# A hybrid GLA and Gated-DeltaNet layer: q and k of GLA as block pairs in seven products, gate dots inside the GDN heads, c spread by TensorE

## The chip, the cores and the metric

The kernel runs on one core of a Trainium2 chip. The metric is the device time of one execution in microseconds. The engines that matter are TensorE (PE, with its weight loads as PEld), VectorE (DVE), ScalarE (ACT), GpSimd (POOL) and SyncE (SP); SP and POOL also issue transfers, each in a queue of its own that it works through in order.

## The reference

The input x has 512 tokens of 2048 channels, c is one row of 2048. All is fp32.

```python
ada = silu(c) @ w_ada + b_ada              # shift, scale, gate: 3 x 2048
h = x * (1 + scale) + shift
q, k, v, g, ..., = split(h @ w_in)         # GLA, GDN, merge gates
# GLA: 4 heads, dk 256, dv 512: S_t = diag(a_t) S_{t-1} + k_t^T v_t, o_t = q_t S_t
# GDN: 16 heads, dk = dv = 128: S_t = a_t (I - b_t k_t k_t^T) S_{t-1} + b_t k_t v_t^T
y = sum over the two branches of sigmoid(merge) * (branch @ w_branch)
out = layernorm(x * alpha + gate * (y @ w_out))
```

What the change touches is the first part of GLA: q and k are each the product of h (512 x 2048) with a 2048 x 1024 matrix, and q is scaled by 1/16. It also touches the 48 tiles of ada: each of its values is a dot product of 2048 channels between silu(c) and one column of w_ada.

## The kernel before, in words

A fp32 product is built from three products of parts: each operand is split in a high part (rounded to the fast matmul's format) and the low rest, and `mm3` (L99 to L102) adds high by high, low by high and high by low. A tile of a projection is 128 output channels by 512 tokens: `proj_col` takes 16 contraction tiles of 3 matmuls, 48 of 512 columns.

Weights come in units of 512 KB (128 x 1024). `unit` (L71) loads a unit on SP's queue into `wraw` (3 buffers, L78), ACT casts it to `whi` (L86), and DVE subtracts to get `wlo` (L88); up to three units are made ahead of PE. Each engine works through its own instructions in order. The order within an engine is settled when the program is built, by a list scheduler that takes the order of the code as priority and a simulated readiness; buffers bound what may be in flight.

The stages, one after the other:

1. Start. silu(c) is spread over 128 partitions by a broadcast load and doubled on DVE (L209); each of the 32 values of shift and scale is a dot product of 2048 elements on DVE (L215) with a 1 MB tile of w_ada. h is made tile by tile: an affine on ACT, then the split (L94, L96). The first 32 steps run eight PSUM banks at a time in three groups of contraction tiles (`steps`, `made`).
2. GDN, 16 heads. `weave` runs a head's steps between the projections' matmuls. Per head: convolutions on DVE (L399, L403), a block solve of 31 rows on DVE (L667, L671) over the buffer `mi`, the state products, and 64 projection steps of PE that cover them. After the solve `mi` is free until the next head.
3. GLA, 4 heads: q and k (four `proj_col`, copied by ACT at L740 and L742), the decays (L746 to L754), the near part of the attention (L344, L350), the row projection of v, the levels (L840), the output, four gate tiles.
4. The gate of ada: 16 dots of 2048 (L215) with loads of 1 MB, between seven tiles of the merge projection.
5. The other merge tiles, the branch products, the output rows, the layer norm.

The projections of merge gates ("merge tiles") depend on h alone. Each ends with a tanh on ACT (L687) and a store to DRAM on SP (L688). A GDN head ends with a store of its output (L630).

## Time and profile before

| what | us |
|---|---|
| median of 3 runs | 2408.9 (2408.81 to 2409.92) |
| the profiled execution | 2410.16 |
| its span | 2408.4 |
| PE busy | 2367.4, 98% of the span, 11788 instructions |
| DVE busy | 1510.7, 63%, 2787 instructions |
| ACT busy | 1054.5, 44%, 1647 instructions |
| POOL busy | 80.3, 3%, 159 instructions |
| PE in the chain that ended last | 90% |

PE is busy from the first matmul to the last stage. The three halves of `mm3` on `pj` make 22, 21 and 21% of the chain that ended last. The granted clock of PE is at its upper level (2.4 GHz) in every one of the 40 slices. DMA is busiest in the first two slices and again in the last quarter, where the transfers of the gate's w_ada and the output rows fall. An idle time is given after an instruction in square brackets, with the engine and the tile that ended it.

### The profile page before, as it was taken

Reading aid. Unit: us, or ns where it says so; the run is one execution under the profiler, and the core shown is the slowest. Engines: PE = TensorE matmul, PEld = TensorE weight load, DVE = VectorE, ACT = ScalarE, POOL = GpSimd, SP = SyncE. Lnnn points to the kernel's source line nnn. Section 1 sums busy time; section 2 is a strip of 40 time slices with the busy share of each in tenths; the row PEclk is TensorE's granted clock in tenths of the full one; section 3 lists DMA queues with packets and bytes.
Section 4 is the critical chain, followed back from the end, with each engine's and each line's share of the span. In section 5 each row is a group of like instructions: output and inputs, shape, how many; then the busy total and the mean of one; then the engine's idle time right before and its main releaser. Section 6 shows DMA issues by size and latency. Waiting matters only on the chain.

```text
span 2408.4 us, 30754 instructions
## 1 busy us (share of the span) xinstructions
PE 2367.4 (98%) x11788; PEld 1943.4 (81%) x11788; DVE 1510.7 (63%) x2787; ACT 1054.5 (44%) x1647; POOL 80.3 (3%) x159
## 2 busy tenths in 40 slices
PE   6999999999999999999999999999999999999997
PEld 5888787888888888878888888888887888888886
DVE  7865677888777788873562745627475322344676
ACT  4335455555665555553442544425424311222353
POOL 0000000000000000000000000000002101010010
PEclk9999999999999999999999999999999999999999
DMA  9964333333333333233223222232298644445674
GB/s 393 369 216 136 114 100 100 100 100 102 100 100 103 108 104 96 96 96 119 94 75 110 88 91 88 76 114 88 92 350 284 214 140 138 146 147 184 215 246 148
DMA packets 119763, 347.92 MB, mean 144 GB/s; under 512 B 32448, under 2 KB 34880, under 8 KB 113472
## 3 DMA queue, kind: packets, MB, share of 16 engines
q1 hardware_dynamic: 109696, 313.45, 38.4%
q0 software_dynamic: 9920, 32.51, 3.9%
q8 instruction: 92, 1.51, 0.3%
q14 instruction: 55, 0.45, 0.1%
HBM read 318.57 MB, written 27.34 MB: 144 GB/s over the span
## 4 chain that ended last, share of the span: by engine, by line
PE 90%; DVE 4%; DMA 3%; issue 1%; ACT 1%; SPq 0%; POOL 0%; POOLq 0%; ACTq 0%; DVEq 0%
PE pj L100 22%; PE pj L101 21%; PE pj L102 21%; PE ms L158 2%; PE ms L157 2%; PE ms L159 2%; PE pj L133 2%; PE pj L134 2%; PE pj L135 2%; PE ms L100 1%; PE ms L102 1%; PE ms L101 1%; PE ms L840 1%; DVE junk L215 1%; DVE wlo L88 1%
## 5 line engine op out<-in xcount | busy, mean ns | idle before, releaser
L100 PE MATMUL pj<-acth,whi 128*128 128x512 f32 x2160 | 870.2, 403 | 20.8 <-ACT acth L94 19.2
L101 PE MATMUL pj<-acth,wlo 128*128 128x512 f32 x2160 | 845.2, 391 | 2.7 <-DVE wlo L88 2.7
L102 PE MATMUL pj<-actl,whi 128*128 128x512 f32 x2160 | 842.8, 391 | 0.0
L88 DVE TENSOR_TENSOR wlo<-wraw,whi 128x1024 fp32r<-128x1024 f32 x414 | 505.1, 1221 | 430.7 <-ACT whi L86 422.6
L86 ACT CAST whi<-wraw 128x1024 fp32r<-128x1024 f32 x414 | 433.7, 1048 | 585.4 <-PE pj L102 383.6
L100 PEld LDWEIGHTS pj<-acth,whi 128*128 128x128 f32 x2160 | 406.7, 188 | 101.4 <-ACT acth L94 20.0
L102 PEld LDWEIGHTS pj<-actl,whi 128*128 128x128 f32 x2160 | 405.9, 188 | 87.4 <-DVE actl L96 0.4
L101 PEld LDWEIGHTS pj<-acth,wlo 128*128 128x128 f32 x2160 | 407.0, 188 | 78.2 <-DVE wlo L88 4.1
L667 DVE TENSOR_TENSOR tmp<-vi,mi 128x8 f32<-128x8 f32 (+30 forms) x496 | 145.9, 294 | 13.3
L671 DVE TENSOR_REDUCE vi<-tmp 128x4 f32<-128x8 f32 (+30 forms) x496 | 111.1, 224 | 13.1
L215 DVE SCALAR_TENSOR_TENSOR junk<-wada,cs 128x2048 f32<-128x2048 f32 x48 | 109.7, 2285 | 4.7 <-DMA wada<-in_wada_dram 4.3
L100 PE MATMUL pj<-yh,whi 128*128 128x512 f32 x256 | 100.9, 394 | 0.0
L101 PE MATMUL pj<-yh,wlo 128*128 128x512 f32 x256 | 100.9, 394 | 0.0
L102 PE MATMUL pj<-yl,whi 128*128 128x512 f32 x256 | 100.9, 394 | 0.0
L158 PE MATMUL ms<-wlo,yh 128*128 128x512 f32 x240 | 94.8, 395 | 0.5 <-DVE wlo L88 0.5
L157 PE MATMUL ms<-whi,yh 128*128 128x512 f32 x240 | 93.8, 392 | 0.0
L159 PE MATMUL ms<-whi,yl 128*128 128x512 f32 x240 | 93.2, 388 | 0.0
L399 DVE SCALAR_TENSOR_TENSOR ac<-upad,convw,ac 128x512 f32<-128x512 f32 x96 | 71.5, 744 | 11.2 <-ACT ac L397 9.6
L133 PE MATMUL pj<-whi,acth 128*128 128x512 f32 x192 | 74.9, 390 | 0.0
L134 PE MATMUL pj<-wlo,acth 128*128 128x512 f32 x192 | 74.9, 390 | 0.0
L135 PE MATMUL pj<-whi,actl 128*128 128x512 f32 x192 | 74.7, 389 | 0.0
L100 PEld LDWEIGHTS pj<-yh,whi 128*128 128x128 f32 x256 | 47.9, 187 | 12.0
(304 smaller groups left out, 2768.8 us busy)
## 6 DMA issues: line engine op xcount, KB each, us to landing
wada<-in_wada_dram SPq DMA_DIRECT2D x48, 1024.0 KB, 8.7
wraw<-in_wqkv_dram SPq DMA_DIRECT2D x90, 512.0 KB, 3.4
wraw<-in_wbr_dram SPq DMA_DIRECT2D x64, 512.0 KB, 3.9
wraw<-in_wout_dram SPq DMA_DIRECT2D x64, 512.0 KB, 4.3
wraw<-in_wmg_dram SPq DMA_DIRECT2D x40, 512.0 KB, 3.6
wraw<-in_wz_dram SPq DMA_DIRECT2D x32, 512.0 KB, 3.5
wraw<-in_wlv_dram SPq DMA_DIRECT2D x32, 512.0 KB, 3.5
wraw<-in_wlg_dram SPq DMA_DIRECT2D x32, 512.0 KB, 3.4
```

The lines of the kernel that those rows point to most:

```text
L86: S.copy(hi, raw)
L88: V.tensor_tensor(lo, raw, hi.bitcast(F32), ALU.subtract)
L100: PE.matmul(ps, wh, ah, start=start, stop=False)
L101: PE.matmul(ps, wl, ah, start=False, stop=False)
L102: PE.matmul(ps, wh, al, start=False, stop=stop)
L133: PE.matmul(pss[c], ah[:, a], hi[:, w], start=kt == 0, stop=False)
L134: PE.matmul(pss[c], ah[:, a], lo[:, w], start=False, stop=False)
L157: PE.matmul(pss[c], ah[:, a], hi, start=kt == 0, stop=False)
L158: PE.matmul(pss[c], ah[:, a], lo, start=False, stop=False)
L159: PE.matmul(pss[c], al[:, a], hi, start=False, stop=kt == KT - 1)
L215: V.scalar_tensor_tensor(junk, wt, 1.0, cs2, ALU.mult, ALU.mult, accum_out=acc_ss[:, j:j + 1])
L667: V.tensor_tensor(tmp[:, :, 0:n], vi[:, :, 0:n], mi[:, 0:n, i:i + 1].rearrange("p s o -> p o s").broadcast_to([P, 4, n]), ALU.mult)
```

## The change

Five things are changed.

GLA's q and k are made in a stage of their own (`qk_all`) between GDN and GLA. A pair of 128-channel blocks, one of q and one of k, is taken as a matrix of 2 x 2 blocks (half the contraction by half the tokens), and is made in seven products instead of eight: four sums of quarters of h are built once (`h_sums`), four differences of weight blocks for every pair (t1 to t4), and the results are added and subtracted on DVE and ACT. Every product is 24 matmuls of 256 columns; a pair is 168, and there are eight pairs. The blocks are loaded into `raw` (six buffers of 512 KB, shared with the sums' inputs). Three merge tiles stand ahead of the pairs in that stage, while h is loaded again on POOL's queue for the sums. Results go to DRAM on POOL's queue and are loaded again in each GLA head.

The gate's 16 dots of 2048 are 32 halves of 1024, two in each GDN head, loaded on POOL's queue into the buffer `mi`. The stage after GLA is gone; its merge tiles stand in other places.

The decays of a GLA head are computed in the head before; those of head 0 stand before one merge tile at the stage's start.

At the start c is loaded as one row and spread by four TensorE matmuls against ones; the dots of the first shift and scale are 32 TensorE matmuls of one column; four matmuls on zeros run before. The first steps are in four groups, and h's high part is written by ACT directly from x.

In the branch stage the loads of GLA's output begin after 45 steps and come every four, where they began after 10 and came every three.

```diff
@@ units @@
-    G1, G2 = 4, 9
-    for lo, hi in ((0, G1), (G1, G2), (G2, KT)):
+    for lo, hi in ((0, 2), (2, 5), (5, 9), (9, KT)):
...
+    NMS, NMG = NMF + 3, NMF + 4
+    use(io["wmg"], range(NMF, NMG))
     for hd in range(HL):
-        for i in range(2):
-            use(io["wlq"], [2 * hd + i])
-            use(io["wlk"], [2 * hd + i])
         use(io["wlv"], [hd], 8)
...
@@ silu_c becomes begin @@
+        crow = room[0:1, 0:4].rearrange("p a t -> p (a t)")
+        nc.sync.dma_start(crow, io["c"])
...
+            wk.append(pool.tile([P, D], F32, name="wada", bufs=4))
+            nc.sync.dma_start(wk[i], io["wada0"][i])
...
+        wait(2)
...
+        for q in range(4):
...
+            PE.matmul(cq, ones1, crow[:, n], start=True, stop=True)
+            S.activation(junk[:, n], cq, AF.Tanh, scale=0.5)
+            V.scalar_tensor_tensor(cs2[:, n], junk[:, n], 1.0, cq, ALU.add, ALU.mult)
...
+                PE.matmul(pd[:, i:i + 1], wk[i][:, k * P:(k + 1) * P], tc_[:, k:k + 1],
+                          start=k == 0, stop=k == KT - 1)
+        wait(2)
...
+            hi = actp.tile([P, T], F32R, name="acth", tag="act", bufs=32)
+            S.activation(hi, xt, AF.Identity, **sc)
...
-        made = [0, 1, 2, 3, 5, 6, 8, 9, 11, 12, 14, 15, 17, 18, 20, 21]
+        made = [0, 0, 2, 4, 5, 7, 8, 10, 11, 13, 15, 16, 18, 19, 21, 22]
...
@@ gdn_all @@
+            def gate_load(j, half):
+                wt = gp.tile([P, D // 2], F32, name="wada", tag="mi", bufs=1)
+                nc.gpsimd.dma_start(wt, io["wada"][32 + j][:, half * D // 2:(half + 1) * D // 2])
+                return j, half, wt
+            def gate_dot(j, half, wt):
+                n = slice(half * D // 2, (half + 1) * D // 2)
+                V.scalar_tensor_tensor(wt, wt, 1.0, cs2[:, n], ALU.mult, ALU.mult,
+                                       accum_out=acc_ss[:, 32 + 16 * half + j:33 + 16 * half + j])
...
+                if hd:
+                    gate_dot(*val["gate"])
+                    val["gate"] = gate_load(hd - 1, 1)
...
+                if hd:
+                    gate_dot(*val["gate"])
                 yield KN
...
+                yield PV + 12
+                val["gate"] = gate_load(hd, 0)
...
@@ qk_all (new) @@
+            for j in range(NMF, NMS):
...
+                for ps in col_steps(h):
+                    if done % 11 == 4 and len(sums) < 4:
+                        h_sums(len(sums))
+                    done += 1
+                merge_store(ps, 12 + j)
...
+            todo = [(p, x) for p in range(8) for x in ("b11", "t1", "t2", "t4", "b21", "b22", "t3")]
+            loads = [(p, x) for p in range(8) for x in ("b11", "b21", "b22", "b12")]
...
+                if x[0] == "t":
+                    a, b = {"t1": ("b12", "b11"), "t2": ("b22", "t1"), "t4": ("b21", "t2"),
+                            "t3": ("b22", "b12")}[x]
+                    src = wp.tile([P, 1024], F32, name="wraw", bufs=3)
+                    V.tensor_tensor(src, raws[p, a], raws[p, b], ALU.subtract)
...
+                load({"t1": 1, "b21": 1, "t3": 2}.get(x, 0))
+            load(RAWS)
...
+                    for k in range(8):
+                        c = slice(k * P, (k + 1) * P)
+                        mm3(ps, hi[:, c], lo[:, c], a[k][0], a[k][1], start and k == 0,
+                            stop and k == 7, skip_group_check=not start)
...
+                product(x, quarter(0, 0), True, True)
+                S.copy(p1, x)
+                product(z, summed(0), True, True)
...
+                nc.gpsimd.dma_start(d_q[hd][:, i], qo)
+                nc.gpsimd.dma_start(d_k[hd][:, i], ko)
...
@@ gla_all @@
-                for i in range(2):
-                    S.activation(q[:, i], proj_col(h), AF.Copy,
-                                 scale=1.0 / 16.0)
-                    S.copy(k[:, i], proj_col(h))
...
+            nxt = (*load_qk(0), decays(0))
+            merge_tile(12 + NMS)
+            for hd in range(HL):
+                q, k, cum = nxt
...
+                if hd + 1 < HL:
+                    nxt = (*load_qk(hd + 1), decays(hd + 1))
...
-    NM = 12 + NMF
-    with tc.tile_pool(name="ada2", bufs=1) as adp:
-        cs2, junk = silu_c(adp)
...
+    qk_all()
...
-                if done > 10 and done % 3 == 0 and len(yl) < KT:
+                if done > 45 and done % 4 == 0 and len(yl) < KT:

```

Where the instructions stand. On DVE, in a GDN head, from the convolution of k on, before:

```order
L399 SCALAR_TENSOR_TENSOR kc<-upad_1500,convw,kc 128x512 [waits DVE_49]
L88 TENSOR_TENSOR wlo<-wraw,whi 128x1024 [waits DMAHW4_49,PE_49,Activation_49]
L399 SCALAR_TENSOR_TENSOR kc<-upad_1500,convw,kc 128x512 [waits DVE_49]
L663 COPY vi<-delta 128x128 [waits DMAHW7_49]
L358 STREAM_TRANSPOSE tc<-vc 128x128 [waits DMAHW0_49]
L358 COPY tf<-tc 32x4x32 [waits DVE_49]
L358 COPY tf<-tc 32x4x32
L403 SCALAR_TENSOR_TENSOR kc<-th,kc 128x512 [waits Activation_49]
L88 TENSOR_TENSOR wlo<-wraw,whi 128x1024 [waits DMAHW5_49,Activation_49]
L358 TENSOR_SCALAR vf_1515<-ms 32x4x32 [waits PE_49]
```

The same place in a head of the changed kernel, from the first convolution (L460) that follows the solve's last read of `mi`:

```order
L460 SCALAR_TENSOR_TENSOR kc<-upad_1587,convw,kc 128x512 [waits Activation_49]
L460 SCALAR_TENSOR_TENSOR kc<-upad_1587,convw,kc 128x512 [waits DVE_49]
L91 TENSOR_TENSOR wlo<-wraw,whi 128x1024 [waits DMAHW1_49,PE_49,Activation_49]
L460 SCALAR_TENSOR_TENSOR kc<-upad_1587,convw,kc 128x512 [waits DVE_49]
L449 SCALAR_TENSOR_TENSOR wada,acc_ss<-wada,cs_1609 128x1024 [waits DMASW0_49]
L401 STREAM_TRANSPOSE tc<-vc 128x128 [waits DMAHW5_49]
L731 COPY vi<-delta 128x128 [waits DMAHW4_49]
L401 COPY tf<-tc 32x4x32 [waits DVE_49]
L401 COPY tf<-tc 32x4x32
L464 SCALAR_TENSOR_TENSOR kc<-th,kc 128x512 [waits Activation_49]
L91 TENSOR_TENSOR wlo<-wraw,whi 128x1024 [waits DMAHW2_49,Activation_49]
L449 SCALAR_TENSOR_TENSOR wada,acc_ss<-wada,cs_1609 128x1024 [waits DMASW1_49]
```

The first half dot (L449) now stands between the last convolution of `kc` and its last product with `th` (L464), and waits for a transfer of POOL's queue; the second stands after the next weight unit (L91), and is followed by the `vf` rows as before.

On SP, at GDN's end, where the stores of merge tiles (`d_mg`) meet the loads of q's and k's weights, before:

```order
L78 DMA wraw<-in_wlq_dram 128x1024 [waits DMAHW6_49,DMAHW3_49,DVE_49]
L78 DMA wraw<-in_wlk_dram 128x1024 [waits DMAHW4_49,DMAHW0_49,DVE_49]
L688 DMA d_mg<-mth 128x512 [waits Activation_49]
L78 DMA wraw<-in_wlk_dram 128x1024 [waits DMAHW1_49,DVE_49]
L78 DMA wraw<-in_wlq_dram 128x1024 [waits DMAHW7_49,DMAHW3_49,DVE_49]
```

The changed kernel, at the end of the three merge tiles ahead of q and k:

```order
L762 DMA d_mg<-mth 128x512 [waits Activation_49] x2
L828 DMA raw<-in_wlq_dram 128x1024 [waits DMASW4_49,DMASW3_49,DMASW5_49,DMASW2_49,DMASW6_49,DMASW1_49,DMASW7_49,DMASW0_49,DMAHW0_49,DVE_49,DMAHW5_49,PE_49,Pool_49]
L762 DMA d_mg<-mth 128x512 [waits DMAHW6_49,Activation_49]
L828 DMA raw<-in_wlq_dram 128x1024 [waits DMAHW7_49,DVE_49]
L828 DMA raw<-in_wlk_dram 128x1024 [waits DVE_49]
L828 DMA raw<-in_wlk_dram 128x1024 [waits DMAHW1_49,DVE_49]
L828 DMA raw<-in_wlq_dram 128x1024 [waits DMAHW2_49,DVE_49]
```

The first block's load is ahead of the store of the last merge tile (the one that waits for ACT), the second to the fourth are behind it.

On PE, the start of the changed kernel (before, the first row was the L100 of `acth` and `whi`):

```order
L224 MATMUL ms<-xt 128x512 [waits Pool_49]
L224 MATMUL ms<-xt 128x512 x3
L235 MATMUL pj<-part,ones_105 128x512 [waits DMAHW0_49,Pool_49]
L235 MATMUL pj<-part,ones_105 128x512 x2
L235 MATMUL ot<-part,ones_105 128x512
L241 MATMUL ms<-tcol,wada 128x1 [waits DMAHW2_49,DVE_49]
L241 MATMUL ms<-tcol,wada 128x1 x15
L241 MATMUL ms<-tcol,wada 128x1 [waits DMAHW3_49]
L241 MATMUL ms<-tcol,wada 128x1 x15
L106 MATMUL pj<-acth,whi 128x512 [waits DVE_49,Activation_49]
```

All four matmuls on zeros are placed first, then four that spread c, then 32 of one column, and only then the first of the projection.

## Rows read from the trace of the kernel before

**Rows 1.** Windows: span; PE, PEld, DVE, ACT, POOL busy (count); clock; DMA; GB/s.

```profile
0.00:240.00 240.00, 220.30 (x963) 181.06 (x964) 174.85 (x227) 103.21 (x146) 4.03 (x19) 1.00 0.73 280
240.00:1060.00 820.00, 817.80 (x4645) 668.67 (x4644) 640.21 (x1658) 462.12 (x892) 8.92 (x14) 1.00 0.33 102
...
1760.00:1850.00 90.00, 87.38 (x382) 71.27 (x381) 59.40 (x69) 26.07 (x34) 9.26 (x18) 1.00 0.84 297
1850.00:2060.00 210.00, 208.87 (x896) 167.25 (x895) 74.15 (x79) 54.22 (x64) 31.61 (x59) 1.00 0.52 181
```

**Rows 2.** Timeline of PE at the start: start us, us, engine, line, operation [idle before].

```profile
16.74 0.79 PE L100 MATMUL pj<-acth,whi 128*128 128x512 f32 x1 [16.74 <-ACT acth L94]
...
22.09 0.55 PE L100 MATMUL ms<-acth,whi 128*128 128x512 f32 x1
```

**Rows 3.** Timeline of ACT, the copies of q and k, GLA head 0.

```profile
1143.38 0.60 ACT L740 ACTIVATE q<-pj 128x512 f32<-128x512 f32 x1 [4.43 <-PE pj L102]
...
1175.97 0.59 ACT L742 COPY k<-pj 128x512 f32<-128x512 f32 x1 [4.38 <-PE pj L102]
```

**Rows 4.** Timeline of PE in GLA's output: matmuls of 256 columns and what follows.

```profile
1243.46 0.28 PE L100 MATMUL ms<-atqf,v 128*128 128x256 f32 x1
...
1243.83 0.38 PE L895 MATMUL ms<-at,v 128*128 128x128 f32 x2
...
1248.19 0.28 PE L100 MATMUL ms<-atqf,v 128*128 128x256 f32 x1
...
1248.54 0.39 PE L895 MATMUL ms<-at,v 128*128 128x128 f32 x2
```

**Rows 5.** One line's instructions (L209): ns min/median/max, first and last start.

```profile
L209 DVE SCALAR_TENSOR_TENSOR cs<-junk,wada x4: 1219/1226/1226, 6.7 to 1751.9; 128x1024 f32<-128x1024 f32 x4
```

**Rows 6.** Timeline in a GDN head: DVE, ACT and PE's weight loads.

```profile
595.94 0.40 DVE L667 TENSOR_TENSOR tmp<-vi,mi 128x128 f32<-128x128 f32 x1
...
599.16 0.74 DVE L399 SCALAR_TENSOR_TENSOR kc<-upad,convw,kc 128x512 f32<-128x512 f32 x1
...
601.01 0.69 DVE L403 SCALAR_TENSOR_TENSOR kc<-th,kc 128x512 f32<-128x512 f32 x1
601.70 1.05 ACT L86 CAST whi<-wraw 128x1024 fp32r<-128x1024 f32 x1
602.78 1.23 DVE L88 TENSOR_TENSOR wlo<-wraw,whi 128x1024 fp32r<-128x1024 f32 x1 [1.08 <-ACT whi L86]
602.79 0.59 PEld L476 LDWEIGHTS ms<-ident,kc 128*128 128x128 f32 x4
...
607.37 0.58 DVE L358 TENSOR_SCALAR vf<-ms 32x128 f32<-32x128 f32 x2 [3.36 <-PE ms L560]
```

**Rows 7.** Two lines' instructions in an early GDN head (L403, L476).

```profile
L403 DVE SCALAR_TENSOR_TENSOR kc<-th,kc x2: 691/692/692, 276.9 to 329.9; 128x512 f32<-128x512 f32 x2
L476 PEld LDWEIGHTS ms<-ident,kc x4: 138/142/143, 277.7 to 278.0; 128*128 128x128 f32 x4
```

**Rows 8.** DMA issues: transfer, queue, count, KB each, median us to landing.

```profile
wraw<-in_wlq_dram SPq DMA_DIRECT2D x16, 512.0 KB, 3.5
...
gt<-d_mg POOLq DMA_DIRECT2D x32, 256.0 KB, 3.2
...
yraw<-d_yl POOLq DMA_DIRECT2D x16, 256.0 KB, 5.6
```

**Rows 9.** Timeline at GDN's end: ACT's tanh and SP's store of a merge tile.

```profile
1132.45 0.60 ACT L687 ACTIVATE mth<-pj 128x512 f32<-128x512 f32 x1
...
1134.26 0.42 SPq L688 DMA_DIRECT2D d_mg<-mth  x1
```

**Rows 10.** Timeline in GLA head 0: decays' matmuls, near's last operand, near's matmul.

```profile
1175.77 0.62 PE L746 MATMUL ms<-lrT,wgk 80*128 80x512 f32 x2
...
1205.93 0.68 DVE L344 TENSOR_TENSOR sql<-e,sqh 128x512 fp32r<-128x512 f32 x1
...
1209.40 0.39 PE L350 MATMUL ms<-sqh,onesr 128*128 128x512 f32 x1
```

More of the change, by code (lines that the diff above doesn't have):

```diff
@@ L89, in unit @@
             ready.append((hi, lo))
+    def unit():
+        fill()
         return ready.pop(0)
@@ L229, in hybrid_layer @@
     with tc.tile_pool(name="ada", bufs=1) as adp:
-        cs2, junk = silu_c(adp)
+        part = adp.tile([P, 16, T], F32, name="part")
+        cs2, junk, pd = begin(adp, part)
+        fill()
         bada = cload("bada", [P, 48])
@@ L681, in gdn_all @@
             first_k = 16 * NMA
+            gcol = gp.tile([P, 16], F32, name="gcol", bufs=1)
             weave([(0, decay())] + [(max(8, first_k + 64 * (hd - 1)), head(hd)) for hd in range(HD)],
                   stream())
+            gate_dot(*val["gate"])
+            gate_dot(*gate_load(HD - 1, 1))
+            V.tensor_tensor(gcol, acc_ss[:, 32:48], acc_ss[:, 48:64], ALU.add)
+            V.scalar_tensor_tensor(gcol, gcol, 0.25, hbgate, ALU.mult, ALU.add)
+            nc.gpsimd.dma_start(d_gate.rearrange("j p -> p j"), gcol)
     def merge_store(ps, j):
```

181 lines of the change are left out of this document (145 added, 36 removed).

## The prediction, made before the changed kernel was run

> **What bounds the kernel now.** I read the windows first, stage by stage, then the timelines at the places where the change puts work. The reader is to see in the windows [rows 1] that PE is the bound: in the GDN stage (240 to 1060 us) it lacks 2.2 us of 820, in the stage of the gate's dots (1760 to 1850) 2.6 us of 90, in the 210 us behind it 1.1 us. Only the start is loose: 19.7 of 240 us, of which 16.74 go by before the first matmul [rows 2]. So there are two kinds of gain, fewer PE microseconds and the idle time of start and gate stage, and two kinds of loss: any wait that the change puts in front of PE counts in full, since PE has nothing in reserve. DVE is at 78% in the GDN stage (640 of 820), so its time is near the edge there [rows 1].
>
> **Part by part.** The sum is made against the profiled execution, 2410.16 us (its span of 2408.4 and 1.8 around it), which lies 1.3 above the median of 2408.9.
>
> *q and k.* Four tiles of 48 matmuls per head end in a copy each; the first copy starts at 1143.38, the fourth at 1175.97, so a tile takes 32.59 / 3 = 10.86 us, and a matmul of 512 columns .2263 [rows 3]. Sixteen tiles: 173.8 us go. What comes is 8 pairs x 7 products x 24 = 1344 matmuls of 256 columns. GLA's output has triples of these with weights of their own: 1243.46 to 1243.83 is .1233 each, 1248.19 to 1248.54 is .1167 [rows 4]. I take .119, near the middle of the two: 159.9 us, a gain of 14. Ends: .1233 gives 165.7 (a gain of 8); half of the 512-column spacing, .113, gives 152.1 (a gain of 22). PE loads new weights ahead of each of these matmuls, twice as often for its columns as in `proj_col`; both triples do that too.
> The Trainium skill ("TensorE: Matmul & The Clock Gate", section "Back-to-back issue gap") gives columns / 2.4 plus 2.5 ns, for 256 columns 109 ns. By that rule the products would take an estimated 147 us, a gain of 27, and the sum below would be some 13 lower. The triples of this trace stand above it, at 117 to 123 ns, and they decide.
>
> *Start.* Before, PE's first 12 matmuls take 22.09 - 16.74 = 5.35 us, where at .2263 they would take 2.7 [rows 2, 3]: 2.6 are lost after the long idle time, though the clock's row reads its upper level. Idle time after the first matmul is 19.7 - 16.7 = 3.0. Together 22.3 us. After, four matmuls on zeros, four that spread c and 32 of one column come first. Unsplit fp32 of 512 columns is not in the trace; its nearest row is .2263, and I bound it by that and four times that, .9; the 32 narrow ones (64 instructions with their passes) by .02 and .12 each. They begin where the zeros and c's row are there, about 6 us (c's product on DVE starts at 6.7 today [rows 5]). Eight of .9 and 64 of .06 are 11 us, so the first useful matmul is at 17, now at full pace, with .6 of later waits: 17.6, a gain of 4.7. Ends: 14.4 when one dot of 2.3 us leaves the chain and nothing else counts (a gain of 8), and twice the pace's price for the first eight, 24 (a loss of 1 to 2).
>
> *Gate stage.* Its waits of 2.62 and part of the 1.13 behind it go [rows 1]: a gain of 3.2; ends 0 and 3.75. The seven merge tiles and the dots' DVE time are moved, not removed.
>
> *GDN heads.* Each has two more half dots of 1.22 us [rows 5] on DVE, and two loads on POOL's queue into `mi`. The first dot stands ahead of `kc`'s last product. That product ends at 601.01 + .69 = 601.70 and PE loads `kc` at 602.79, so a head has 1.09 of slack [rows 6]; the head at 276.9 has .1 [rows 7]. The delay is 1.24 with slack taken off: .15 per head at the one end, 1.14 at the other, over 15 heads 2 to 17 us. Most heads repeat like the one of [rows 6], so I take .3, and 4.5 in all. The second dot stands behind the weight unit that ends at 604.01; DVE is idle from there until `vf` at 607.37 [rows 6]: it is hidden, up to 2 us late. If the first dot has to wait for its load, everything behind waits too: `mi` is read last until 596.34, the dot comes at 599.90, so a landing within 3.55 us costs nothing [rows 6]. On SP 512 KB land in 3.5 us; on POOL half as much in 3.2 where queues are quiet, in 5.6 in the branch stage [rows 8]. I take 3.5, since the GDN stage's DMA share is a third [rows 1], and keep 5.6 for the rivals.
> Queued behind the waiting dot on DVE are `kc`, a weight unit and `vf`; PE waits for `kc` first. On POOL the second load waits for the first dot.
>
> *Entry of the new stage.* After GDN, three merge tiles of 10.86 keep PE until 32.6 us (from the stage's start). The loads of the second to fourth weight block stand on SP behind the last merge tile's store, and that one waits for a tanh of .60; the store itself takes SP .42 [rows 9]. The fourth block, b12, is in t1, which the second product needs. Three loads from 33.7 on: 3.5 for one [rows 8], and two more at 512 KB / 354 GB/s (297 at a share of .84 [rows 1]) = 1.5 each: it lands at about 40.1. Then the difference (as a subtract, 1.23), the cast 1.05, the subtract 1.23 [rows 6]: 43.6. The first product ends at 32.6 + 24 x .119 = 35.5, so PE waits 8 us. Ends: 2 where only the store's turn is lost, 12 where PE loses 2.6 after the gap as at the start and the third product is late too. I take 8.
>
> *Behind that entry* DVE has per pair seven subtracts and four differences of 1.22 and some 1.8 of additions, 15.2 us, against 168 x .119 = 20 of PE: hidden.
>
> *GLA head 0.* The decays' matmuls start at 1175.77, near's second ones matmul at 1209.40, 33.6 us later; its operand is ready at 1206.61, slack 2.8 [rows 10]. After, these matmuls stand 38 into v's 192, so 38 x .2263 = 8.6 us of cover are gone: 5.8 at most. The copies of q and k and the cumulative sums no longer queue there, so I take half, 3. Ends 0 and 7. Later heads have decays a head ahead, which can't cost PE time there.
>
> Sum: -14 - 4.7 - 3.2 + 4.5 + 8 + 3 = -6.4, so 2403.8 for the profiled execution and 2402.5 for the median; I say 2402.
>
> **The rivals.**
> - *Slower: the gate's first load lands late on POOL's queue.* At 5.6 us, as for yraw [rows 8], each of 15 heads waits 2.05 more at a place without slack: +31, so 2433. From a landing of about 4.0 the sum is no gain (15 x .43 = 6.4), from 4.3 it is measurably slower. For it: the transfer is twice the size of those in the two POOL rows, and DVE is at 78% in that stage [rows 1]. Against: DMA is idle two thirds of the stage, and SP lands as much in 3.5 [rows 8].
> The Trainium skill ("SBUF — State Buffer", section "SBUF: two separate sides") warns that a transfer issued by GpSimd stands still while VectorE runs an operation that holds both port pairs, as its descriptors can't be written. No row of this kernel shows a transfer of POOL under a DVE as busy as in a GDN head; by the rule the landing would be at the late end, which is this rival.
> - *No change.* The entry costs 12, head 0 costs 7, GDN 7: the gain of 22 is eaten, about 2409. For it: each is a PE wait in a kernel whose PE has no reserve; against: the three must all go wrong.
> - *Slower: DVE bounds the products.* Four of seven products need a difference, a cast and a subtract, 3.5 us one after the other, where PE needs 2.9; without the three units made ahead this is .6 x 32 = +20, so 2422. Against: ACT and DVE work at different units in turn.
> - *Faster: the products run at half the 512-column time,* .113, and the entry is filled by other work: -8 and -8, so 2386.
>
> **How the numbers follow.** Differences under .2% (4.8 us) can't be told from no change: faster is below 2404.1, slower above 2413.7. Forecast .50 (own range 2394 to 2409: faster .35, same .15); faster rival .18; no change .12 (same .09, slower .03); late load .13 (same .02, slower .11); DVE-bound products .07 (same .01, slower .06). Together: faster .53, same .27, slower .20. The range 2384 to 2416 holds the faster rival and the beginnings of a late load (up to a wait of 1 us in each head), and leaves out the two slower rivals' full price.
>
> **What would show it.** q and k: 168 matmuls of a pair at 19 to 21 us, and .119 between starts. Start: the first `acth` matmul at about 17, and the next 12 at .23. GDN: PE's waits for `kc` add to 4.5 us, and for the dots' loads to none; a landing above 4 on POOL speaks for the first rival. Entry: one gap on PE of about 8 us between the first and the second product, ended by the difference's split. GLA head 0: a wait of some 3 us for near's operand. Gate stage: no wait of PE for a DMA behind GLA. The prediction is wrong if PE's idle time in the GDN stage grows beyond 15 us, or if the products' spacing lies outside .113 to .124.

## The result: 2441.9 us, slower by 1.3%

The changed kernel takes 2441.85 us in the median (2437.35 to 2443.29, 4 runs), the kernel before 2409.41 beside it: a ratio of 1.0132 [1.0119, 1.0145]. The forecast was 2402, at most 2416: wrong in sign.

The profiled execution takes 2440.97, its span is 2438.7, 30.3 more than before. Three stretches tell most of it. The windows of the changed kernel (columns as in [rows 1]; the third is the stretch with the new q and k stage, 1150 to 1360):

```profile
0.00:240.00 240.00, 235.88 (x1003) 191.03 (x1004) 177.47 (x237) 100.08 (x142) 7.50 (x23) 0.96 0.73 275
240.00:1060.00 820.00, 810.48 (x4581) 659.36 (x4579) 665.33 (x1699) 460.33 (x887) 24.92 (x44) 1.00 0.37 120
1150.00:1360.00 210.00, 202.20 (x1529) 194.00 (x1528) 151.27 (x162) 97.68 (x123) 18.74 (x36) 0.98 0.43 150
```

PE is busier at the start than in [rows 1] and yet the clock there reads .96: busy is not progress. In the GDN stage PE now lacks 9.5 us of 820 where it lacked 2.2. The account, by the same events in both traces:

| stretch, from event to event | change, us | forecast |
|---|---|---|
| start, to the first head's `kc` (212.03 to 221.37) | +9.3 | -4.7 |
| GDN, from there to the end of its last merge tile | +7.5 | +4.5 |
| q and k products, steady (19.52 a pair for 21.7) | -17.8 | -14 |
| entry of their stage | +12.4 | +8 |
| rest of that stage | +1.7 | |
| merge tile ahead of head 0 | +2.3 | |
| four GLA heads, without q and k (434.4 to 454.75) | +20.3 | +3 |
| behind GLA, without the four merge tiles that moved ahead (624.3 to 618.8) | -5.5 | -3.2 |
| sum | +30.2 | -6.4 |

**Start.** PE's timeline of the changed kernel (columns as in [rows 2]):

```profile
1.32 6.62 PE L224 MATMUL ms<-xt 128*128 128x512 f32 x8 [1.32 <-POOL xt L217]
7.87 2.84 PE L235 MATMUL pj<-part,ones 1*128 1x512 f32 x6
10.55 1.80 PE L235 MATMUL ot<-part,ones 1*128 1x512 f32 x2
12.29 13.81 PE L241 MATMUL ms<-tcol,wada 128*128 128x1 f32 x64
27.45 0.79 PE L106 MATMUL pj<-acth,whi 128*128 128x512 f32 x1 [1.35 <-ACT acth L286]
28.04 0.63 PE L107 MATMUL pj<-acth,wlo 128*128 128x512 f32 x1
...
30.75 0.57 PE L107 MATMUL pj<-acth,wlo 128*128 128x512 f32 x1
```

Its windows of 10 us (PE busy, clock, DMA share, GB/s):

```profile
10.00:20.00 10.00, 10.00 (x41) 0.53 0.88 358
20.00:30.00 10.00, 8.65 (x35) 0.50 0.57 201
```

The 64 records of one column take 13.81 us, .216 each, at half the granted clock, 1.2 GHz. The reader is to see that PE is 100% busy at that clock. The trace's clock records give half the clock from 10.65 to 31.13 us, so it fell 1.6 us before the first narrow matmul (12.29). The run e_dots_dve, below, has no narrow matmuls, and there the clock is at half from 9.66 to 26.73. So the narrow matmuls did not bring it down. It falls between 9.3 and 12.2 us in every profiled run with the new start and in none with the old one; what in the new start does it is not shown. What a narrow matmul costs at either clock shows in e_own, where the fall comes at 12.10 (windows of its narrow matmuls alone; PE and weight loads busy, then DVE and ACT, clock, DMA):

```profile
10.52:12.10 1.58, 1.58 (x14) 1.58 (x15) 0.00 (x0) 0.00 (x0) 1.00 1.10 428
12.10:22.90 10.80, 10.80 (x52) 10.73 (x51) 0.00 (x0) 0.00 (x0) 0.50 0.81 335
```

They start .11 apart at the upper clock and .213 apart at the lower. The first useful matmul of the changed kernel comes at 27.45 instead of 16.74 [rows 2], and the first eight of 512 columns are mostly .43 apart, not .2263.

**Products.** The first copy of each pair (ACT; `p`) gives the pair's time:

```profile
1216.59 0.37 ACT L870 COPY p<-pj 128x256 f32<-128x256 f32 x1 [0.39 <-PE pj L108]
1236.11 0.37 ACT L870 COPY p<-ms 128x256 f32<-128x256 f32 x1 [0.43 <-PE ms L108]
```

19.52 us / 168 = .1162 a matmul, the lower of the two triples in [rows 4]. Eight pairs are 156.2 for 173.8 to 174, where 159.9 was forecast.

**A GDN head.** Timeline of the changed kernel at the place of [rows 6]:

```profile
659.92 0.40 DVE L735 TENSOR_TENSOR tmp<-vi,mi 128x128 f32<-128x128 f32 x1
660.62 0.55 POOL L444 DMA_DIRECT2D wada<-in_wada_dram  x1 [21.23 <-DVE tmp L735]
...
665.30 1.23 DVE L449 SCALAR_TENSOR_TENSOR wada<-wada,cs 128x1024 f32<-128x1024 f32 x1 [1.42 <-DMA wada<-in_wada_dram]
667.27 0.69 DVE L464 SCALAR_TENSOR_TENSOR kc<-th,kc 128x512 f32<-128x512 f32 x1
668.02 0.66 PE L540 MATMUL ms<-ident,kc 128*128 128x128 f32 x4 [0.79 <-DVE kc L464]
```

The load is issued .3 after the last read of `mi`, the dot starts 4.7 after that issue begins, and DVE stands still for 1.42 ahead of it, with `kc` behind. In 13 of 15 heads the first dot waits (.21 to 1.44, 10.3 us in all). PE's waits from 240 to 1060 us, first of the changed kernel, then of before (total, times, longest):

```profile
PE ms L540 <- DVE kc L464: 8.7, 11, 1.1
```

```profile
PE ms L476 <- DVE kc L403: 1.9, 1, 1.9
```

**Entry of the q and k stage.** PE and ACT of the changed kernel, where the last merge tile ends and the first product starts:

```profile
1181.51 0.39 PE L108 MATMUL pj<-actl,whi 128*128 128x512 f32 x1
1183.66 1.99 ACT L799 CAST sh<-raw 128x1024 fp32r<-128x1024 f32 x2 [1.12 <-DVE raw L791]
1185.56 1.04 ACT L843 CAST whi<-raw 128x1024 fp32r<-128x1024 f32 x1
1186.65 0.58 PE L106 MATMUL ms<-acth,whi 128*128 128x256 f32 x1 [4.75 <-ACT whi L843]
1188.29 0.58 PE L107 MATMUL ms<-acth,wlo 128*128 128x256 f32 x1 [1.05 <-DVE wlo L845]
1188.66 0.41 PE L108 MATMUL ms<-actl,whi 128*128 128x256 f32 x1
1188.88 0.41 PE L106 MATMUL ms<-acth,whi 128*128 128x256 f32 x1
...
1194.22 0.35 PE L106 MATMUL ms<-sh,whi 128*128 128x256 f32 x1 [1.45 <-issue]
```

The main gap is ahead of the first product, not behind it, and what ends it is ACT's cast of the first block, which stands behind the casts of h's sums (`sh`). Of 7.8 us of waits up to the third product, 5.8 are ahead of the first product and just behind its first matmul, and 2.0 are at the second product. The rest of the 12.4 is the lower clock behind them: .213 between starts where .116 follows.

**A GLA head.** PE's waits of the changed kernel, first from 1355 to 1380 us, then the longest from 1370 to 1825:

```profile
PE pj L139 <- ACT mth L761: 3.2, 1, 3.2
```

```profile
PE ms L393 <- ACT sqh L385: 6.7, 3, 2.6
```

The first is head 0's `v`, which waits for the bank of the merge tile ahead of it.

Its timeline of ACT and PE in head 1:

```profile
1550.40 1.28 ACT L949 ACT_TABLE_LOAD   x1
1551.69 0.63 ACT L949 ACTIVATE t<-t 128x512 f32<-128x512 f32 x1
1553.03 0.59 ACT L1104 COPY of<-ms 128x512 f32<-128x512 f32 x1 [0.71 <-PE ms L1103]
...
1564.63 0.62 ACT L385 CAST sqh<-total 128x512 fp32r<-128x512 f32 x1
1565.31 0.50 PE L393 MATMUL ms<-sqh,onesr 128*128 128x512 f32 x1 [2.01 <-ACT sqh L385]
```

And the kernel's windows of 4 us there (columns as in [rows 1]):

```profile
1561.00:1565.00 4.00, 2.29 (x11) 1.56 (x9) 3.96 (x6) 3.97 (x6) 0.00 (x0) 1.00 0.00 0
1565.00:1569.00 4.00, 3.22 (x9) 2.32 (x10) 4.00 (x6) 3.97 (x5) 0.00 (x0) 0.77 0.00 0
1569.00:1573.00 4.00, 4.00 (x15) 3.17 (x15) 3.99 (x5) 3.97 (x6) 0.00 (x0) 0.81 0.39 131
```

The next head's decays (L947 to L949, with table loads) stand among this head's output copies on ACT, ACT and DVE are full, and PE waits for the norm's operand `sqh`; then the clock reads .77 and .81. The table loads have moved, not multiplied: GLA has 24 before, 24 here and 24 in e_own. Heads 0 to 3 take 119.6, 114.2, 113.3 and 107.7 us, before 110.2 and three times some 108.05: the last, which has no next head, is level.

### The profile page after: what moved, and what is told of

Its sections match the earlier page's. It is cut to its first block, busy times and chain, and to the rows that moved or that the text cites. A ratio compares the mean times of both kernels' runs of the same rounds, so it can differ in the third digit from the quotient of the medians.

```text
span 2438.7 us, 32492 instructions
## 1 busy us (share of the span) xinstructions
PE 2387.3 (98%) x12444; PEld 1978.0 (81%) x12444; DVE 1610.9 (66%) x2938; ACT 1100.6 (45%) x1716; POOL 123.2 (5%) x236
## 5 line engine op out<-in xcount | busy, mean ns | idle before, releaser
L106 PE MATMUL pj<-acth,whi 128*128 128x512 f32 (+1 forms) x1968 | 787.9, 402 | 1.9 <-ACT acth L286 1.4
L107 PE MATMUL pj<-acth,wlo 128*128 128x512 f32 (+1 forms) x1968 | 763.0, 388 | 0.9 <-DVE wlo L91 0.9
L108 PE MATMUL pj<-actl,whi 128*128 128x512 f32 (+1 forms) x1968 | 762.4, 388 | 0.0
L91 DVE TENSOR_TENSOR wlo<-wraw,whi 128x1024 fp32r<-128x1024 f32 x382 | 465.4, 1220 | 345.7 <-ACT whi L89 341.6
L108 PEld LDWEIGHTS pj<-actl,whi 128*128 128x128 f32 x1968 | 370.9, 188 | 78.2 <-DVE actl L290 0.7
L106 PEld LDWEIGHTS pj<-acth,whi 128*128 128x128 f32 x1968 | 371.8, 189 | 70.5 <-ACT acth L286 1.4
L107 PEld LDWEIGHTS pj<-acth,wlo 128*128 128x128 f32 x1968 | 372.2, 189 | 66.5 <-DVE wlo L91 1.5
L106 PE MATMUL ms<-acth,whi 128*128 128x512 f32 (+1 forms) x224 | 77.2, 348 | 4.8 <-ACT whi L843 4.8
L107 PE MATMUL ms<-acth,wlo 128*128 128x512 f32 (+1 forms) x224 | 77.7, 347 | 1.1 <-DVE wlo L845 1.1
L460 DVE SCALAR_TENSOR_TENSOR ac<-upad,convw,ac 128x512 f32<-128x512 f32 x96 | 71.5, 744 | 10.6 <-ACT ac L458 9.5
L108 PE MATMUL ms<-actl,whi 128*128 128x512 f32 (+1 forms) x224 | 77.6, 346 | 0.0
```

Of the source, the lines that this page charges most:

```text
L91: V.tensor_tensor(lo, raw, hi.bitcast(F32), ALU.subtract)
L106: PE.matmul(ps, wh, ah, start=start, stop=False, **kw)
L107: PE.matmul(ps, wl, ah, start=False, stop=False, **kw)
L108: PE.matmul(ps, wh, al, start=False, stop=stop, **kw)
```

## Experiments

Each is the changed kernel with one edit unless it says otherwise. "Span" is the profiled execution's. The same start code showed its first useful matmul at 24.3 in some executions and at 27.45 in others (the clock rises earlier and falls later there: 5.27 and 12.10 us in e_own for 7.24 and 10.65), so a span's difference below 3 us is read by stage only.

**e_dots_dve**: the first shift and scale again as dots on DVE; zeros, spread of c and four groups stay.

```diff
-            if kt:
-                ada_dot(adp, cs2, junk, kt)
-                ada_dot(adp, cs2, junk, KT + kt)
+            ada_dot(adp, cs2, junk, kt)
+            ada_dot(adp, cs2, junk, KT + kt)
```

> The changed kernel, with only the first shift and scale dots back on DVE (as for every other tile); c is still spread by TensorE, the four matmuls on zeros and the four groups of steps stay. Theory A (the 64 records of one column cost a weight load each, .216 us at the lower clock, 13.8 us in a row, and the projection starts at 27.45 behind them): two DVE dots of 2.29 take their place behind the spread that ends at 13.7, the first acth matmul comes at 19 to 21, and the whole is 6 to 9 us faster than the changed kernel's 2441.9, so about 2434. Rival B (the start is late through the loads or the clock, whatever does the dots): first acth matmul later than 25, the whole within 3 us of 2442.

2436.03, ratio 1.011 [1.0095, 1.0125]. The first useful matmul comes at 20.87, the first `kc` at 215.72 for 221.37: the 64 narrow matmuls cost 5.7 of the start's 9.3.

**e_start_old**: the whole start as before (three groups, c by DMA, no zeros).

```diff
-    for lo, hi in ((0, 2), (2, 5), (5, 9), (9, KT)):
+    for lo, hi in ((0, 4), (4, 9), (9, KT)):
...
-        cs2, junk, pd = begin(adp, part)
+        cs2, junk = silu_c(adp)
```

> The changed kernel with the start of the kernel before: broadcast load of c, all dots on DVE, three groups of steps, no matmuls on zeros. Theory A (the new start is slower by its 64 records at one weight load each, and gains nothing that the old one hasn't): first acth matmul at 16.7, the first head's kc at 212 to 213 instead of 221.4, the whole 8 to 10 us faster than the changed kernel's 2441.9, about 2433; also faster than the one with only the dots moved back (2436, kc at 215.7). Rival B (the spread of c and the four groups do help once the dots are off PE): 2436 or more, kc at 215 or more.

2432.82, ratio 1.0099 [1.0084, 1.0114]. First useful matmul:

```profile
16.43 0.79 PE L106 MATMUL pj<-acth,whi 128*128 128x512 f32 x1 [16.43 <-ACT acth L100]
```

The first `kc` is at 212.84. The start's loss is the new start's, all but .8; which part of it, beyond the 5.7 of the narrow matmuls, was not tried apart.

**e_nogate**: leaves out the gate's dots, their loads and the spread of c for them.

```diff
-                    gate_dot(*val["gate"])
-                    val["gate"] = gate_load(hd - 1, 1)
...
+            G.memset(acc_ss[:, 32:64], 0.0)
```

> The changed kernel without the gate's 16 dots: their loads, their 32 half dots and the spread of c for them are left out of the GDN heads, zeros stand in their place. Theory A (the dots and their late loads on POOL's queue delay kc and what is behind it on DVE, some .6 us a head): the time from the first head's kc to the sixteenth's goes from 831.4 back to about 822.6, the whole is 8 to 10 us faster than 2441.9, so about 2433. Rival B (the heads grew for another cause, such as the shifted start or POOL's queue order): the span between the first and last kc stays at 829 or more and the whole within 3 us of 2442.

2439.58, ratio 1.0115 [1.01, 1.013]. From the first `kc` to the 16th 831.46, as with the dots (831.40): missed. But its first head has a wait of 5.5 for `kc` that the changed kernel has not (69.2 us for 62.9), in a head that the scheduler, without the dots, orders in another way. From the second head's `kc` to the sixteenth's it is 762.3, for 768.5 with the dots and 757.7 before. That is no clean answer.

**e_gate_noload**: the dots stay, over a buffer already there; the loads of w_ada for the gate are left out, and with them its values.

```diff
-                wt = gp.tile([P, D // 2], F32, name="wada", tag="mi", bufs=1)
-                nc.gpsimd.dma_start(wt, ...)
+                wt = cs2[:, half * D // 2:(half + 1) * D // 2]
```

> The changed kernel with the 32 half dots of the gate in place but without their loads: they read a tile that is already there (the loads of the gate's w_ada are left out, and the gate's values with them), so they neither wait for POOL's queue nor share mi. Theory A (the wait for the first load, .2 to 1.5 us a head, and mi's sharing are most of the heads' growth): kc from the second to the sixteenth head takes 758 to 762 us instead of 768.5. Rival B (DVE's time of 2 x 1.3 us a head is the growth): 765 or more, waits for kc still 7 to 9 us.

2454.75, ratio 1.0191 [1.0171, 1.0211]. With nothing to wait for, the dots came all between 220 and 294 us, in the first heads (the second to the fourth take 66.2, 56.7, 63.7 us), and PE waited 11.1 for `tc`. The run moved the dots as well as leaving out the loads, so it doesn't separate load from dot.

**e_gate_later**: dots and loads stay; the first dot is issued behind `kc`, the second behind `um`.

```diff
+                    with tc.issue_after(val[hd, "k", "ins"]):
+                        gate_dot(*val["gate"])
...
+                    with tc.issue_after(um_.ins):
+                        gate_dot(*val["gate"])
```

> The changed kernel with both gate dots of a head moved on DVE: the first behind kc's last product, the second behind the product um; loads and buffer stay. Theory A (PE's 8.7 us of waits for kc come from the first dot ahead of it; leaving the dots out altogether removed these waits too, but met one other wait of 5.5 us in the first head): the waits for kc fall under 3 us, and kc from the second to the sixteenth head takes 758 to 761 us instead of 768.5; the whole 6 to 10 us faster than 2441.9, about 2434. Rival B (DVE's amount of work in a head is the limit, wherever the dots stand): the waits move to vf or to the state's products, 766 or more, no gain.

2447.06, ratio 1.0154 [1.0137, 1.017]: missed; from the first `kc` to the 16th 838.45. No dot of a head waits for its load now, and PE's waits for `kc` fall only to 5.7. DVE waits for the loads `cB` (17.5 us, 12 times) and `vc` (15.7, 14 times) instead. Behind `kc` is no better place; what exactly the heads lose there was not followed.

**e_gate_own**: the loads get a buffer of their own and are issued a slot ahead; for its room only half of c's row is kept, and the second half is loaded midway.

```diff
-                wt = gp.tile([P, D // 2], F32, name="wada", tag="mi", bufs=1)
+                wt = gp.tile([P, D // 2], F32, name="gw", bufs=1)
...
+                if slot == 15:
+                    spread(1)
+                if slot < 31:
+                    val["gate"] = gate_load(slot + 1)
```

> The changed kernel with the gate's half dots at the same places on DVE, but with a buffer of their own for the loads, each issued as soon as the dot before it is done (room for it: c's row is kept half at a time). Theory A (the wait for the first load is what PE loses; the dot's own 1.3 us fits kc's slack): the first dots no longer wait, PE's waits for kc fall under 3 us, kc from the second to the sixteenth head takes 758 to 761 us instead of 768.5, and the whole is 7 to 10 us faster than 2441.9. Rival B (the dot's own time is the loss): no wait for the loads, but kc's waits stay at 6 us or more and the heads at 765 or more.

2436.0, ratio 1.0104 [1.0087, 1.0121]. Its dots stand at the same places; two of one head:

```profile
657.97 1.22 DVE L451 SCALAR_TENSOR_TENSOR gw<-gw,cs 128x1024 f32<-128x1024 f32 x1
...
663.45 1.23 DVE L451 SCALAR_TENSOR_TENSOR gw<-gw,cs 128x1024 f32<-128x1024 f32 x1 [1.28 <-DMA gw<-in_wada_dram]
```

The first dot waits in no head; the second still waits 1.3, without adding to the heads' time. PE's waits for `kc` are 2.6 in two places. From the second head's `kc` to the sixteenth's it is 766.4, where 758 to 761 were expected: the two heads around the spread of c's second half take 59.9 and 56.8. The other twelve take 54.1 in the mean, for 54.9 in the changed kernel and 54.1 before. So the heads' growth was the wait for the landing, not the dot's 1.23 us; e_best3, which spreads c's second half elsewhere, bears it out. Of the 5.9 that the whole gains on the changed kernel, some 2.6 are the quicker kind of start (24.27).

**e_entry4**: four merge tiles ahead of the pairs, not three.

```diff
-    NMS, NMG = NMF + 3, NMF + 4
+    NMS, NMG = NMF + 4, NMF + 5
```

> The changed kernel with four merge tiles instead of three ahead of the pairs (one fewer in the branch stage). Theory A (the sums of h are a chain of four groups of 6.8 us on ACT and DVE that ends 4 us after the third tile, and the first block's cast stands behind it; then the wait for b12): one more tile of 10.9 us covers most of the 12.4 us lost there, and nothing is missed later; 8 to 11 us faster than 2441.9, so about 2432. Rival B (the loads of the second to fourth block stand behind the last tile's store, wherever that is): the wait of the second product stays, only the first one's 5.8 us go with their slow clock: about 2437.

2427.08, ratio 1.007 [1.0053, 1.0087], 14.8 below the changed kernel. The stage, less the fourth tile's 10.86, falls by 12.2, and PE waits for nothing in it; `v`'s wait for `mth` at GLA's start stays, 4.0. The entry's 12.4 was cover that was missing.

**e_decays_late** and **e_decays_mid**: the next head's decays are issued at the third, and at the second, of the head's four gate tiles (the second also puts the merge tile ahead of head 0's decays).

```diff
-                if hd + 1 < HL:
-                    nxt = (*load_qk(hd + 1), decays(hd + 1))
...
+                    if j == 2 and hd + 1 < HL:
+                        nxt = (*load_qk(hd + 1), decays(hd + 1))
```

> The changed kernel with the next GLA head's loads of q and k and its decays moved from ahead of the output to the third gate tile, behind the output's norm. Theory A (the decays' ACT work, with its table loads, stands ahead of the output's copies and squares on ACT, so the norm's ones matmuls wait and PE then runs at the lower clock): the three heads that do it, at 114 to 120 us, come down to about 108, and the whole is 12 to 17 us faster than 2441.9, so about 2427. Rival B (the heads are longer because q and k come back from DRAM, or because near's operands are late): the heads stay above 112, and the whole within 4 us of 2442.

> The changed kernel with the next head's loads and decays at the second gate tile (not ahead of the output, and not at the third as in the run before, where they delayed the last gate tile's product and v had to wait 3.1 us for its bank), and the merge tile ahead of the first head's decays instead of behind them. Theory A (both waits are ACT and DVE queues at one place; in the middle of the gate tiles they have slack): heads 1 to 3 take 108 to 109 us each, head 0 under 112, the whole 15 to 19 us faster than 2441.9, about 2425. Rival B (v has no cover between gate tiles and itself since q and k went, so any decays there delay it): heads stay at 112 or more, about 2437.

2442.67, ratio 1.0126 [1.0111, 1.0141], and 2438.53, ratio 1.0123 [1.0108, 1.0138]: missed. In e_decays_late PE's waits for `sqh` are gone and another has come:

```profile
PE pj L139 <- DVE th L1117: 9.4, 3, 3.1
```

At either place PE waits for `th` instead, 9.4 and 8.3 us in all; heads 0 to 2 stay at 112 to 120.

**e_own**: each head's decays at its own start; q and k are still loaded a head ahead.

```diff
-                q, k, cum = nxt
+                q, k = nxt
+                cum = decays(hd)
```

> The changed kernel with each GLA head's decays at the head's own start, ahead of v's 192 matmuls, as before the change (the loads of q and k stay a head ahead); the first head's too, behind the merge tile. Theory A (computed a head ahead, wherever put, the decays and the next head's near work that they release queue on ACT and DVE in front of something PE needs soon: the output's norm, or the last gate tile's product that frees v's bank; at the head's own start v's 43 us cover them): heads 1 to 3 take 108 to 110 us, no wait of 3 us for th, 8 to 12 us faster than the changed kernel's 2441.9, about 2432. Rival B (without q and k between the gate tiles and v the head has lost its slack, so the decays cost near's operands or v's bank even there): heads of 113 or more, within 4 us of 2442.

2423.17, ratio 1.0053 [1.0038, 1.0068], 18.7 below, of which some 2.6 are the quicker kind of start. The heads take 114.3, 109.4, 109.0, 107.5; GLA 440.2 for 454.75. PE's longest waits in GLA:

```profile
PE pj L139 <- ACT mth L761: 4.9, 1, 4.9
PE ms L108 <- DVE atGt L1089: 2.6, 3, 1.2
```

The waits for `sqh` are gone. The first line is `v` of head 0 behind the merge tile. In e_best3, where that tile has another bank, the wait is gone and head 0 takes 110.4, as before's 110.2.

**e_all**: e_start_old, e_entry4, e_gate_later and e_decays_mid together.

> The seven products and the gate's dots in GDN kept; start as before, gate dots behind kc and um, four merge tiles ahead of the pairs, decays at the second gate tile, merge tile ahead of the first decays. If the losses found are separate and each is undone here, the sum is -9 (start) -8 (heads) -12 (entry) -17 (GLA) from 2441.9: about 2396, 13 us faster than the kernel before, near what the seven products (14 to 18) and the gate stage (4 to 5) are worth. Rival B (losses move from one place to the next, as with the third gate tile): 2410 or more.

2433.93, ratio 1.01 [1.0084, 1.0116]: two of the four edits had been no cure alone, and the GDN stage grows to 845.9.

**e_best_gdn**: e_start_old, e_entry4 and e_own together.

> Seven products, gate's dots in the GDN heads as in the changed kernel; start as before, four merge tiles ahead of the pairs, each head's decays at its own start. Theory: the three losses are separate: 2441.9 - 9 - 12 - 10 = about 2411; with the heads' growth of 9 still in, level with the kernel before. Rival (the GLA heads keep their loss): 2420 or more.

2409.49, ratio .9994 [.9985, 1.0004]: level with before. Undoing the three gives 32.4 us of 32.4. By stage they give 34.4 (start 8.6, entry 12.2, GLA 13.6), and the GDN stage takes 2.8 back: PE's waits for `kc` are 10.5 here. Singly the three whole times fell by 42.5, more than together.

**e_best_back**: e_best_gdn with the gate's dots behind GLA, as before, between four of the merge tiles that are left; the branch stage's loads begin and come as before, too.

> As the one before, but with the gate's dots in a stage of their own behind GLA, as before the change, with four of six merge tiles between them. Theory A (the GDN heads go back to 757.7 us between the second and the sixteenth kc, a gain of 10; the gate's stage costs 4 to 8 again): about 2405, faster than the kernel before by what the seven products leave. Rival B (the stage with four tiles between the dots instead of seven waits for 16 MB of w_ada, 40 us, in full): 2412 or more.

2431.14, ratio 1.0091 [1.0075, 1.0108]. The GDN stage is back at 822.53, but PE waits behind GLA:

```profile
PE pj L106 <- ACT whi L89: 10.1, 2, 8.4
PE pj L106 <- issue: 5.0, 1, 5.0
```

16 MB of w_ada have 4 tiles of cover, where before they had seven. Whether that or the branch stage's loads make the waits was not tried apart.

**e_best2**: e_best_gdn with e_gate_own's buffer, the dots behind `kc` and `um`, and the merge tile ahead of head 0 in another bank.

> Start as before, four merge tiles ahead of the pairs, decays at each GLA head's own start (2409.5 with the gate's dots as changed), and now the loads with a buffer of their own, the first dot behind kc's last product and the second behind um, and the merge tile ahead of the first GLA head in another bank, so that v does not wait for its tanh. Theory A: the heads take 758 us between the second and the sixteenth kc (10 us gained), v's wait of 3.6 and the slow clock behind it go (5 us): about 2396, clearly faster than the kernel before. Rival B (DVE's amount of work in a head is the limit wherever the dots stand, as the run with moved dots and shared buffer suggested): heads at 768 or more, 2405 or more.

2443.37, ratio 1.0136 [1.0121, 1.0151]. PE waits 23.5 us for `st` in 14 places of the GDN stage: behind `kc` the dots cost PE time even where the loads have a buffer of their own.

**e_best3**: e_best_gdn with e_gate_own's buffer, dots at the changed kernel's places, c's second half spread behind `um` in one head, and the merge tile ahead of head 0 in another bank.

```diff
+                if hd == 8:
+                    with tc.issue_after(um_.ins):
+                        spread(1)
+                    val["gate"] = gate_load(16)
```

> Start as before, four merge tiles ahead of the pairs, decays at each GLA head's own start, the merge tile ahead of the first GLA head in another bank; gate's dots at the changed kernel's places (the first ahead of kc's last product), with a buffer of their own for the loads; c's second half spread behind um in one head. Theory A (what PE lost in the heads was the wait for the first load, not the dot's time): kc from the second to the sixteenth head takes 758 to 762 us, and the whole comes to 2409.5 - 8 (heads) - 5 (v's wait and the slow clock behind it) = about 2397, 12 us faster than the kernel before. Rival B (the version with moved dots lost 27 us in waits for the state st; DVE is too full in a head for 2.6 us more anywhere): heads at 766 or more, 2405 or more.

2408.13, ratio .9993 [.9984, 1.0002]. From the second head's `kc` to the sixteenth's it is 761.3, but the last two dots stand in the last head's chain:

```profile
PE ms L625 <- DVE st L362: 9.5, 1, 9.5
```

**e_best4**: e_best3 with these two behind the last solve and the last output.

```diff
+            with tc.issue_after(val["solved"]):
+                gate_dot(*val["gate"])
+            with tc.issue_after(val["end"]):
+                gate_dot(*val["gate"])
```

> The version before, with the last two of the 32 half dots behind the last head's solve and behind its output, instead of in the middle of the last head where PE waited 9.5 us for the state st behind them. Theory: that wait and the slow clock behind it (10 to 13 us) go and nothing takes their place; the last tile of the GDN stage ends at 1095 to 1098 instead of 1107.8, and the whole comes to about 2397, 12 us faster than the kernel before, which is the value of the seven products with everything else level. Rival: the second of them, behind the output, delays the sums of h and with them the first pairs: 2403 or more.

2412.27, ratio 1.0014 [1.0004, 1.0024]. GDN ends at 1135.69, 3.2 behind before; the gain is lost in the next stage. POOL's timeline:

```profile
1138.93 1.18 POOL L732 DMA_DIRECT2D d_gate<-gcol  x1 [50.55 <-DVE gcol L731]
1152.22 4.26 POOL L759 DMA_DIRECT2D raw<-in_xT_dram  x8 [12.10 <-PE pj L108]
```

The gate's store holds the heads' memory for 12 us (8 KB in single numbers; before, on SP, it took 12.2), and x's loads for the sums go into that memory.

**e_best5**: e_best4 with the store's source among the constants, and the store itself at the end of the code (POOL still issues it first).

```diff
+    gcol = cst.tile([P, 16], F32, name="gcol")
...
-            gcol = gp.tile([P, 16], F32, name="gcol", bufs=1)
...
-            nc.gpsimd.dma_start(d_gate.rearrange("j p -> p j"), gcol)
...
+    with tc.issue_after(later[-1]):
+        nc.gpsimd.dma_start(d_gate.rearrange("j p -> p j"), gcol)
```

> The kernel of e_best4 with the gate row's column (the scattered store's source) kept among the constants, so that the heads' memory no longer waits for that store and the first loads of the sums' columns are free to land before it. Theory A (the store that held the heads' memory is what cost e_best4 its entry): the loads for the sums land some 10 us earlier than at 1152, the q/k stage comes back from 216.5 us to 202 to 206, and the time is 2398 to 2405, faster than before. Rival B (the entry is bound by the chain of the sums itself, or the store still stands ahead on its queue): the stage stays at 212 to 217 and the time at 2409 to 2414.

2408.79, ratio .9990 [.9981, .9999].

```profile
1140.78 1.18 POOL L1107 DMA_DIRECT2D d_gate<-gcol  x1 [50.55 <-DVE gcol L733]
1142.23 3.73 POOL L760 DMA_DIRECT2D raw<-in_xT_dram  x7 [0.27 <-issue]
1155.64 0.54 POOL L760 DMA_DIRECT2D raw<-in_xT_dram  x1 [9.68 <-DMA raw<-in_xT_dram]
```

Seven of eight loads come 10 us earlier, the eighth does not. From GDN's end to the last q of the stage it is 210.9 us for 216.6, where e_best_gdn has 201.7. Theory A was right in kind and gave half its size; what holds the rest of that entry was not tried apart. No version beat the kernel before by more than a measurement tells: this one is .1% below, with an interval that ends at .9999.

## Why the prediction was wrong

*Products: right*, .1162 for .119, -17.8 for -14. *Gate stage: right in sign*, -5.5 for -3.2, but outside its ends of 0 to 3.75; the later loads of the branch stage are in it too and were not tried apart.

*Start: the failed step is "64 of .06".* No row stood behind its bounds of .02 and .12. The records take .216, nearly four times the term and above the bound, because the granted clock was at 1.2 GHz; at the upper clock they are .11 apart (e_own), inside the bound but still nearly twice the term. "Eight of .9" was short as well: PE begins at 1.32, not at 6, and the zeros and c's spread take it until 12.3. So 1.3 + 11.0 + 13.8 and a wait of 1.35 make the 27.45. "Now at full pace" failed too: the clock had risen by 7.2 and fallen again at 10.65, and the next eight matmuls are .43 apart. The prediction read the clock's row of the kernel before at its upper level there; that trace has no clock record ahead of 22.42, and up to that time the matmuls of [rows 2] keep the lower clock's distance of .43. By e_dots_dve the narrow dots are 5.7 of the 9.3.

*GDN heads: the mechanism was named, as the slower rival, and set to nothing in the sum.* "A landing within 3.55 us costs nothing; I take 3.5": the median landing on POOL is 3.8, and with the issue the first dot comes 4.98 us after the last read of `mi` (665.30 - 660.32). The waits add to 10.3, and the stretch from the second head's `kc` to the sixteenth's grew by 10.8; e_gate_own takes the first dots' waits away with the buffer. The first head gained 1.9 and the end of the stage 1.4 against it, so the term is 7.5. That lies inside the 2 to 17, but by luck: the 4.5 was meant for the dot's own time, which costs next to nothing in e_gate_own. The 5.6 us that the rival priced (+31) did not occur. The Trainium skill ("SBUF — State Buffer", section "SBUF: two separate sides") warns of a POOL transfer that stands still while VectorE runs an operation in a mode that takes both port pairs. With DVE at 81% in that stage and landings of 3.8 us, no such standstill shows in this trace for the operations that DVE runs here.

*Entry: 8 forecast, 12.4 measured, for another reason.* "One gap between the first and the second product, ended by the difference's split" is wrong in the main: 5.8 of the 7.8 us of waits are the first product's, for ACT behind the sums of h, and 2.0 the second's. The prediction counted loads and one block's split, not the four groups of sums that ACT, DVE and `raw`'s buffers have to get through first. The lower clock after the wait made some 4.6 of it.

*GLA: the step "later heads have decays a head ahead, which can't cost PE time there" failed.* It looked at PE alone. The decays' activations, with a table load each time the function changes, stand on an ACT that is 3.97 of 4 us busy, and what PE needs next queues behind them. e_own takes 14.5 us out of GLA. For head 0 the +3 was to be a wait for near's operand; that wait (`sql`) is .2 in e_own. What keeps head 0 there 4.1 above before is `v`'s wait of 4.9 for the merge tile's bank, so its size inside the 0 to 7 is luck.

Of +32.4 us, undoing start, entry and decays ahead removes all (e_best_gdn). The landing in the GDN stage is another 7.5, and GLA is still 6.7 above before in e_best_gdn; the products' gain pays for these.

## What to carry to other kernels

Where one engine is the bound, a move is priced on the queues of the others too: ask what stands behind the moved work on ACT or DVE, and who is fed by that. Loading into a buffer whose last reader is just ahead of the use makes the landing part of every pass; slack of a few hundredths over the median landing is none. Several edits that each shift the order don't add: undo them one at a time and together.

## What the hardware showed unexpectedly

With the new start the clock read half for 17 to 24 us, from 9.3 to 12.2 us on, while PE was 100% busy (the changed kernel, 10 to 20 us) as well as when it was 24% busy (e_dots_dve, the same window). With the old start, where PE idles until 16.4 to 17.1 us, no such fall is recorded, though the first matmuls are .43 apart there too, until 22.1 us in the kernel before. What brings the fall about is open. A clock row of 1.00 ahead of the trace's first clock record says nothing of the clock.

The waits of 2 to 5 us on PE in the GLA head and at the entry were followed by some microseconds at .77 to .81, or at .213 between 256-column matmuls instead of .116, so they cost more than their length (7.8 us became 12.4 at the entry). A store of 8 KB in single numbers held its source for 12 us, and with it the memory of a whole stage.
